# mLSTM scores in a hybrid decoder step: queries and their remainder side by side, one product of 256 columns a block

## The chip, the cores and the metric

The kernel runs on one core of a Trainium2 chip. A core has five engines that run on their own and meet through semaphores: TensorE (matmul; PE in the profile, its weight loads PEld), VectorE (DVE), ScalarE (ACT), GpSimd (POOL) and SyncE (SP, which here issues the DMAs). TensorE reads its operands from the on-chip memory SBUF and writes to the accumulator memory PSUM, which has eight banks of 512 fp32 columns; VectorE and ScalarE read PSUM and SBUF. The metric is the device time of one execution, in microseconds, as the median of several runs.

## The reference

One step of a 4-layer decoder trunk for a prompt of 512 tokens and 8 samples of 4 tokens each, all with width 1024. Layers 0 and 3 mix tokens with an mLSTM matrix memory, layer 1 with gated linear attention, layer 2 with sliding-window attention; each is followed by a convolutional feed-forward block. The part of the mLSTM mixer that the change touches, for the prompt, is the score product `qk` of a chunk (8 heads, 64 key channels a head):

```
logw = a[:, None, :, :] + (f_cum - m_t)[:, :, None, :]
w = jnp.where(causal, jnp.exp(jnp.minimum(logw, 0.0)), 0.0)
qk = jnp.einsum('bthd,bshd->btsh', q, k) * w
...
num = jnp.einsum('btsh,bshv->bthv', qk, v) + g[..., None] * jnp.einsum('bthd,bhdv->bthv', q, c)
den = jnp.sum(qk, axis=2) + g * jnp.einsum('bthd,bhd->bth', q, n)
h = num / jnp.maximum(jnp.abs(den), jnp.exp(-m_t))[..., None]
```

All arithmetic is fp32.

## The kernel before

**Number types.** TensorE takes a rounded fp32 type (fp32r). To keep fp32 accuracy, an operand is split into a rounded part and a remainder, and a product is made of several matmuls. All large matrices go this way: line 191 (ScalarE) makes the rounded weights `wh`, line 192 (VectorE) the remainder `wl`, and `gemm` (line 263) runs three products for each of two halves of 272 columns into the accumulator `acc`. Every matmul call stands at line 164, every transpose at line 167.

**Banks and scratch.** PSUM is divided into two double banks named `acc` (pool `psA`) for the large products, and four banks named `m` (pool `psM`) for everything else: scores, outputs of heads, carry, decode, transposes. SBUF has a pool of eight scratch tiles named `t`.

**Order of the work.** The program is written as one stream: `gemm` calls `tick` after each part, and `tick` advances generators (`attention`, line 902) that emit the token mixer's instructions in between. A planner then orders all instructions: it plays the program through with its own costs, takes of the instructions that can start the one that comes first in the program, and gives out tile buffers as they come free; weight conversions and evacuations (lines 190 and 243) get a raised priority. The order it finds is fixed for each engine; on the chip each engine works through its own list in order and waits on semaphores.

**mLSTM heads.** The prompt's 512 tokens are cut into four blocks of 128. For head `h`, with the heads of a pair in the two halves of 64 partitions:

- `decays(h)` (line 699) makes the weights `w` of the four blocks, 128x512, in the scratch tile `SW[h]`: four VectorE instructions (line 704) and an exponential on ScalarE (line 706).
- `prep(h)` (line 754) splits queries and keys. The 128 partitions hold 64 channels twice: `ks` has the rounded keys in one half and their remainder in the other, `qs` the rounded queries in both halves, `ql` the queries' remainder in both. So one matmul of `ks` against `qs` gives rounded and remainder keys times rounded queries, and one against `ql` the same for the remainder of the queries. There is one buffer of each (`bufs=1`), 128x512.
- `scores(h)` (line 767) takes one bank `m`; for each block two matmuls of 128 columns go to the same quarter of it, and the second accumulates on the first. VectorE multiplies the bank with `SW[h]` in place (line 774).
- `av(h)` (line 789) multiplies `SW[h]` with the values and the carried state into two banks, and works out norms and denominators: line 801 reads the denominators, line 783 squares (ScalarE, four a head), line 806 writes the scaled outputs and is the last to read the two banks.
- For each pair of heads, `carry_in` (line 716) transposes keys into a bank and weighs them, and `carry` (line 734) makes the state of the four blocks in two banks (sixteen narrow matmuls, read by lines 745 and 748). `dec_scores` and `dec_av` (lines 819 and 837) do the samples' tokens, `dec_av` with one bank.

Within the loop of `attention`, for each head: decode queries and scores (even heads), `decays` and `prep` of the next head, `carry_in` (odd heads), `av(h)`, then `scores(h + 1)`, behind it `carry` (odd heads) or, a tick later, `dec_av` (even heads), and at last `finish(h)`, which transposes the outputs. For each layer the first scores and the first carry come ahead of the loop.

Of the kernel before, what the change touches and what calls it, by code (L numbers as in the profile page):

```python
# [11 lines left out]
F32R = mybir.dt.float32r  # L12
I32 = mybir.dt.int32
AF = mybir.ActivationFunctionType
ALU = mybir.AluOpType
# [5 lines left out]
NP = 512  # L21
# [91 lines left out]
class Step:  # L113
# [433 lines left out]
    def mlstm(self, L, j):  # L547
        nc, a, tc = self.nc, self.a, self.tc
        ctx = ExitStack()
        mp = self.mp = ctx.enter_context(tc.tile_pool(name=f"mx{L}", bufs=1))  # L550
# [28 lines left out]
        Q, K = {}, {}  # L579
# [116 lines left out]
        SW = {}  # L696
# [55 lines left out]
        KQ = {}  # L752

        def prep(h):
            r = slice(64 * (h % 2), 64 * (h % 2) + 64)
            o = slice(64 - 64 * (h % 2), 128 - 64 * (h % 2))
            q, k = Q[h // 2][r, 0:NP], K[h // 2][r, 0:NP]
            ks, qs, ql = [mp.tile([128, NP], F32R, tag=x, name=x) for x in ("ks", "qs", "ql")]
            nc.scalar.activation(ks[r], k, AF.Copy)
            nc.scalar.activation(qs[r], q, AF.Copy)  # L760
            nc.scalar.activation(qs[o], q, AF.Copy)
            nc.vector.tensor_tensor(out=ks[o], in0=k, in1=ks[r].bitcast(F32), op=ALU.subtract)
            nc.vector.tensor_tensor(out=ql[r], in0=q, in1=qs[r].bitcast(F32), op=ALU.subtract)
            nc.scalar.activation(ql[o], ql[r].bitcast(F32), AF.Copy)
            KQ[h] = (ks, qs, ql)

        def scores(h):
            ks, qs, ql = KQ.pop(h)
            s = self.m()
            for i in range(4):  # L770
                c = slice(128 * i, 128 * i + 128)
                self.mm(s[:, c], ks[:, c], qs[:, c], True, False)
                self.mm(s[:, c], ks[:, c], ql[:, c], False, True)
            nc.vector.tensor_tensor(out=SW[h], in0=s, in1=SW[h], op=ALU.mult)

        def hnorm(num, den, ss, em, sc, cols, p, tag):

# [124 lines left out]
        def attention():  # L902
# [5 lines left out]
            yield 2  # L908
            decays(0)
            prep(0)  # L910
            carry_in(0)
            load_na(1)
            yield 2
            scores(0)
            yield 2
            carry(0)
            yield 2
            for h in range(8):
# [6 lines left out]
                if h + 1 < 8:  # L925
                    while ("qk", (h + 1) // 2) not in done:
                        yield 1
                    decays(h + 1)
                    prep(h + 1)
                    if h % 2:  # L930
                        carry_in(p + 1)
# [4 lines left out]
                if h + 1 < 8:  # L936
                    yield 1
                    scores(h + 1)
                    if h % 2:
                        carry(p + 1)  # L940
# [895 lines left out]
```

## Time and profile before

| | us |
|---|---|
| median of 3 runs | 2587.24 (2584.53 to 2589.8) |
| profiled execution | 2587.89 |
| its span, first to last instruction | 2586.1 |
| TensorE busy | 2554.6 (99%) |
| VectorE busy | 1594.1 (62%) |
| ScalarE busy | 1103.4 (43%) |
| GpSimd busy | 218.5 (8%) |

The busy time of an engine is the time in which at least one of its instructions runs; matmuls overlap, so that a matmul's own duration (some 0.28 us) is longer than the distance between the starts of two. In a row of a group, the figures behind the bar are busy time in us, mean duration of one in ns, and the idle time of the engine just before them with what ended it. In a row of a timeline, the first figure is the start in us from the span's start, the second the time from the start of the first to the end of the last of the merged instructions, and brackets at the end hold the idle time before it and what ended it. A row of waits names the waiting engine, its tile and line, behind the arrow the one that it waited for, then the total in us, how often, and the longest.

### The profile page before, as it was taken

The page shows a single profiled execution, that of the slowest core. Times are in us where ns is not written, and L with a number is a line of the kernel's source. Part 1 is how long each engine was busy: PE and PEld are TensorE (multiplying, and loading weights), DVE is VectorE, ACT ScalarE, POOL GpSimd, SP SyncE. Part 2 cuts the span into 40 slices and gives each one's busy share as a digit, 9 for nine tenths or more (in the row PEclk, how much of TensorE's full clock was granted, in tenths as well). Part 3 has the DMA queues.
Part 4 walks back from the last instruction along what each step waited for, and adds up shares of the span by engine and source line. Part 5 has one row for each costly group of instructions (what it writes and reads, how often), then busy time and mean ns, then how long its engine had stood idle before and what let it go on. Part 6 is the DMA issues. An engine that isn't in the chain of part 4 may idle for free.

```text
span 2586.1 us, 52775 instructions
## 1 busy us (share of the span) xinstructions
PE 2554.6 (99%) x21207; PEld 2499.3 (97%) x21207; DVE 1594.1 (62%) x3401; ACT 1103.4 (43%) x2092; POOL 218.5 (8%) x571
## 2 busy tenths in 40 slices
PE   8999999999999999999999999999999999999998
PEld 7999999999998899999999999999999999999998
DVE  5677775545457666564557865464555777756464
ACT  5544433334455543232347743232345544423232
POOL 2110000001002200000010000000010110000000
PEclk9999999999999999999999999999999999999999
DMA  5333333233222224433332223323333332333332
GB/s 178 105 106 81 91 111 103 84 93 99 74 79 88 91 84 143 139 92 88 88 115 67 69 71 89 87 87 90 86 101 101 100 93 82 111 111 85 91 85 81
DMA packets 137573, 247.24 MB, mean 96 GB/s; under 512 B 16528, under 2 KB 32400, under 8 KB 137296
## 3 DMA queue, kind: packets, MB, share of 16 engines
q1 hardware_dynamic: 135888, 242.26, 32.3%
q8 instruction: 167, 2.74, 0.4%
q10 hardware_dynamic: 1440, 1.60, 0.2%
q14 instruction: 78, 0.64, 0.1%
HBM read 230.89 MB, written 14.94 MB: 95 GB/s over the span
## 4 chain that ended last, share of the span: by engine, by line
PE 93%; DVE 4%; ACT 1%; issue 1%; DMA 1%; POOL 1%; DVEq 0%; SPq 0%; POOLq 0%; ACTq 0%
PE acc L164 81%; PE m L164 11%; PE m L167 1%; POOL s L544 0%; DVE wl L192 0%; DVE t L704 0%; ACT junk L783 0%; DMA out_a_cso<-st 0%; DVE t L513 0%; DMA XT<-in_x 0%; DVE sg L987 0%; DVE st L869 0%; ACT wh L191 0%; DVE t L1096 0%; DMA sd<-in_b_s 0%
## 5 line engine op out<-in xcount | busy, mean ns | idle before, releaser
L191 ACT ACTIVATE wh<-wr 128x512 fp32r<-128x512 f32 (+2 forms) x776 | 482.4, 623 | 1080.2 <-PE acc L164 986.3
L164 PE MATMUL acc<-XH,wh 128*128 128x272 f32 x3744 | 786.8, 291 | 0.0
L164 PE MATMUL acc<-XH,wl 128*128 128x272 f32 x3744 | 776.2, 288 | 0.0
L164 PE MATMUL acc<-XL,wh 128*128 128x272 f32 x3744 | 775.1, 288 | 0.0
L192 DVE TENSOR_TENSOR wl<-wr,wh 128x512 fp32r<-128x512 f32 (+2 forms) x776 | 523.4, 675 | 314.1 <-ACT wh L191 310.1
L164 PEld LDWEIGHTS acc<-XH,wh 128*128 128x128 f32 x3744 | 587.2, 188 | 8.3 <-issue 6.0
L164 PEld LDWEIGHTS acc<-XL,wh 128*128 128x128 f32 x3744 | 588.3, 188 | 1.0 <-issue 0.8
L164 PEld LDWEIGHTS acc<-XH,wl 128*128 128x128 f32 x3744 | 586.2, 189 | 1.1 <-issue 0.8
L164 PE MATMUL acc<-HH,wh 128*128 128x272 f32 x1920 | 404.5, 290 | 1.7 <-DVE sg L987 1.5
L164 PE MATMUL acc<-HL,wh 128*128 128x272 f32 x1920 | 399.1, 288 | 0.2 <-DVE HL L344 0.2
L164 PE MATMUL acc<-HH,wl 128*128 128x272 f32 x1920 | 398.7, 288 | 0.0
L164 PEld LDWEIGHTS acc<-HH,wh 128*128 128x128 f32 x1920 | 302.2, 188 | 4.8 <-DVE sg L987 2.0
L164 PEld LDWEIGHTS acc<-HL,wh 128*128 128x128 f32 x1920 | 302.4, 188 | 0.5 <-DVE HL L344 0.5
L164 PEld LDWEIGHTS acc<-HH,wl 128*128 128x128 f32 x1920 | 301.4, 189 | 0.0
L530 DVE TENSOR_TENSOR XT<-acc,XT 128x544 f32<-128x544 f32 x158 | 114.2, 723 | 137.9 <-PE acc L164 136.5
L443 POOL COPY cc<-t 128x2 f32<-128x2 f32 x88 | 54.6, 620 | 1283.9 <-DVE t L441 1278.7
L440 DVE TENSOR_TENSOR t<-acc,rb 128x272 f32<-128x272 f32 x88 | 38.9, 442 | 143.4 <-PE acc L164 140.7
L164 PE MATMUL m<-wh,XH 128*128 128x256 f32 (+1 forms) x400 | 115.5, 290 | 7.1 <-ACT XH L346 6.6
L164 PE MATMUL m<-wl,XH 128*128 128x256 f32 (+1 forms) x400 | 114.6, 287 | 1.0 <-DVE wl L192 1.0
L164 PE MATMUL m<-wh,XL 128*128 128x256 f32 (+1 forms) x400 | 114.6, 287 | 0.0
L455 DVE TENSOR_TENSOR t<-acc,t 128x544 f32<-128x544 f32 x88 | 63.7, 723 | 70.5 <-PE acc L164 69.9
L446 ACT ACTIVATE t<-t,par 128x560 f32<-128x560 f32 x88 | 75.4, 857 | 51.2 <-DVE t L442 51.2
(359 smaller groups left out, 2616.7 us busy)
## 6 DMA issues: line engine op xcount, KB each, us to landing
wr<-in_w SPq DMA_DIRECT2D x700, 256.0 KB
wr<-in_w SPq DMA_DIRECT2D x64, 192.0 KB
st<-in_a_cs SPq DMA_DIRECT2D x16, 520.0 KB
sd<-in_b_s SPq DMA_DIRECT2D x32, 256.0 KB
out_a_cso<-st SPq DMA_DIRECT2D x8, 520.0 KB
na<-scr SPq DMA_DIRECT2D x16, 256.0 KB
out_b_so<-sd SPq DMA_DIRECT2D x16, 256.0 KB
wr<-in_w SPq DMA_DIRECT2D x12, 272.0 KB
```

Of the source, the lines that this page charges most:

```text
L164: self.nc.tensor.matmul(out, lhsT=lhsT, rhs=rhs, start=start, stop=stop, skip_group_check=True, **kw)
L167: self.nc.tensor.transpose(out, in_, self.ident[0:k, 0:k])
L191: self.nc.scalar.activation(hi[:, 0:n], raw[:, 0:n], AF.Copy)
L192: self.nc.vector.tensor_tensor(out=lo[:, 0:n], in0=raw[:, 0:n], in1=hi[:, 0:n].bitcast(F32), op=ALU.subtract)
L440: nc.vector.tensor_tensor(out=g[:, 2:274], in0=acc[:, 0, 0:HT], in1=rb[:, 0:HT], op=ALU.mult)
L443: nc.gpsimd.tensor_copy(cout[:, f, 0:2], g[:, 512:514])
L446: nc.scalar.activation(c, g[:, 2:562], AF.Identity, scale=self.par[:, pw + 2:pw + 3], bias=self.par[:, pb:pb + 1])
L455: nc.vector.tensor_tensor(out=self.h2(h), in0=acc[:, :, 0:HT], in1=self.h2(s2), op=ALU.mult)
L530: self.nc.vector.tensor_tensor(out=self.h2(x), in0=acc[:, :, 0:HT], in1=self.h2(x), op=ALU.add)
```

## The change

`qs` and `ql` become the two halves of one tile `qq`, 128 x 4 blocks x 2 x 128: for each block the rounded queries and their remainder stand side by side. `ks` gets the shape 128 x 4 x 128. The six preparing instructions stay, with the new views as outputs. `scores` takes two banks, one for two blocks each: a block is one matmul of 256 columns, whose first 128 results come from the rounded queries and the second 128 from the remainder. The sum of the two, made by the second matmul's accumulation before, is made outside: ScalarE copies the remainder's half out of the bank into a new scratch tile `w`, VectorE adds the other half of the bank to it, each once a bank; then VectorE multiplies `w` with `SW[h]`.

```diff
         def prep(h):
             r = slice(64 * (h % 2), 64 * (h % 2) + 64)
             o = slice(64 - 64 * (h % 2), 128 - 64 * (h % 2))
-            q, k = Q[h // 2][r, 0:NP], K[h // 2][r, 0:NP]
-            ks, qs, ql = [mp.tile([128, NP], F32R, tag=x, name=x) for x in ("ks", "qs", "ql")]
+            q, k = [x[h // 2][r, 0:NP].rearrange("p (c x) -> p c x", c=4) for x in (Q, K)]
+            ks = mp.tile([128, 4, 128], F32R, tag="ks", name="ks")
+            qq = mp.tile([128, 4, 2, 128], F32R, tag="qq", name="qq")
+            qs, ql = qq[:, :, 0], qq[:, :, 1]
             nc.scalar.activation(ks[r], k, AF.Copy)
             nc.scalar.activation(qs[r], q, AF.Copy)
             nc.scalar.activation(qs[o], q, AF.Copy)
             nc.vector.tensor_tensor(out=ks[o], in0=k, in1=ks[r].bitcast(F32), op=ALU.subtract)
             nc.vector.tensor_tensor(out=ql[r], in0=q, in1=qs[r].bitcast(F32), op=ALU.subtract)
             nc.scalar.activation(ql[o], ql[r].bitcast(F32), AF.Copy)
-            KQ[h] = (ks, qs, ql)
+            KQ[h] = (ks, qq)
 
         def scores(h):
-            ks, qs, ql = KQ.pop(h)
-            s = self.m()
-            for i in range(4):
-                c = slice(128 * i, 128 * i + 128)
-                self.mm(s[:, c], ks[:, c], qs[:, c], True, False)
-                self.mm(s[:, c], ks[:, c], ql[:, c], False, True)
-            nc.vector.tensor_tensor(out=SW[h], in0=s, in1=SW[h], op=ALU.mult)
+            ks, qq = KQ.pop(h)
+            w = self.t(512).rearrange("p (a x) -> p a x", a=4)
+            for half in range(2):
+                s = self.m().rearrange("p (a b x) -> p a b x", a=2, b=2)
+                for i in range(2):
+                    c = 2 * half + i
+                    self.mm(s[:, i].rearrange("p b x -> p (b x)"), ks[:, c], qq[:, c].rearrange("p b x -> p (b x)"), True, True)
+                w2 = w[:, 2 * half:2 * half + 2]
+                nc.scalar.copy(w2, s[:, :, 1])
+                nc.vector.tensor_tensor(out=w2, in0=s[:, :, 0], in1=w2, op=ALU.add)
+            nc.vector.tensor_tensor(out=SW[h], in0=w.rearrange("p a x -> p (a x)"), in1=SW[h], op=ALU.mult)
```

## The prediction

> **What bounds the kernel now.** I read the page's busy rows and its chain first, then a table by stage for the two stretches in which the mLSTM heads are worked on, and then the waits of TensorE.
>
> ```profile
> span 2586.1 us, 52775 instructions
> PE 2554.6 (99%) x21207; PEld 2499.3 (97%) x21207; DVE 1594.1 (62%) x3401; ACT 1103.4 (43%) x2092; POOL 218.5 (8%) x571
> PE 93%; DVE 4%; ACT 1%; issue 1%; DMA 1%; POOL 1%; DVEq 0%; SPq 0%; POOLq 0%; ACTq 0%
> ```
> ```profile
> core 0: us, PE busy (x) PEld busy (x) DVE busy (x) ACT busy (x) POOL busy (x), PEclk, DMA share, GB/s
> 75.00:225.00 150.00, 146.95 (x1231) 140.02 (x1230) 108.23 (x313) 72.40 (x174) 18.25 (x23) 1.00 0.35 100
> 1990.00:2130.00 140.00, 136.94 (x1151) 130.01 (x1150) 101.82 (x299) 65.84 (x162) 16.87 (x21) 1.00 0.35 95
> ```
> ```profile
> PE m L164 <- DVE t L774: 2.5, 4, 1.1
> ```
>
> The reader sees a kernel that is TensorE's own stream of matmuls: 99% busy, 93% of the chain, and 147 of 150 us in the mLSTM stretch of layer 0. So whatever shortens that stream shortens the kernel one for one, and whatever makes TensorE wait lengthens it one for one. The clock is full in these stretches, so it is no variable. VectorE (108 of 150 us) and ScalarE (72 of 150) have room. The last row is where the changed code already touches TensorE: four times it stands still, 2.5 us in all, until the multiplication at line 774 has read the score bank. Each layer's stretch repeats the same order of instructions, so what happens once per layer counts twice.
>
> **The change, part by part.**
>
> *Matmuls.* Before, one head's scores are eight matmuls of 128 columns; the start times tell what one costs, since a matmul's own duration overlaps the next one's.
>
> ```profile
> 89.65 0.22 PE L164 MATMUL m<-qs,ks 128*128 128x128 f32 x1
> 89.71 0.27 PE L164 MATMUL m<-ql,ks 128*128 128x128 f32 x1
> ...
> 90.37 0.28 PE L164 MATMUL m<-ql,ks 128*128 128x128 f32 x1
> 90.49 0.46 PE L164 MATMUL acc<-XH,wh 128*128 128x272 f32 x2
> ```
> ```profile
> L164 PE MATMUL m<-qs,ks x64: 220/273/277, 89.6 to 2114.1; 128*128 128x128 f32 x64
> L164 PE MATMUL m<-ql,ks x64: 272/275/280, 89.7 to 2114.2; 128*128 128x128 f32 x64
> ```
>
> From 89.65 to 90.49 is 0.84 us for eight, some 0.11 us a step, and there are (64 + 64) / 8 = 16 such sets, eight in each mLSTM layer. What a 256-column step of the same number type costs stands in the attention layer, where the stationary side changes each time, as it will here:
>
> ```profile
> 1379.62 0.28 PE L164 MATMUL m<-KEL,qs 128*128 128x256 f32 x1
> ...
> 1381.26 0.27 PE L164 MATMUL m<-KOL,qs 128*128 128x256 f32 x1
> 1381.37 0.29 PE L164 MATMUL acc<-XH,wh 128*128 128x272 f32 x1
> ```
>
> From 1379.62 to 1381.37 these are 15 steps (the thirteen rows left out are of the same kind) in 1.75 us, 0.117 us each. A step of 256 columns thus costs hardly more than one of 128, and four of them cost 0.47 us. The saving is 0.84 - 0.47 = 0.37 us a set, 16 x 0.37 = **5.9 us**. Six sets are followed by the carry's narrow products and take 0.93 us (193.62 to 194.55 below); if the extra 0.09 us belongs to the scores, the saving is 6 x 0.09 = 0.5 us more. I take **6.2**, between 5.9 and 6.5. The number of weight loads falls with the matmuls; they lie beside them and are in the step already.
>
> One rule of the Trainium skill speaks against this term. "TensorE: Matmul & The Clock Gate", section "Back-to-back issue gap", gives the spacing of isolated matmuls as columns over 2.4 GHz plus 2.5 ns, an estimate of 56 ns for 128 columns and 109 ns for 256; by it eight narrow ones cost 0.45 us, four wide ones 0.44 us, and the change saves nothing. The trace disagrees: 0.84 us for the eight. The same page's section "LDWEIGHTS (loading the stationary operand)" charges a load of 128 columns with columns over 1.2 GHz, 107 ns, which as a floor under both kinds would give an estimate of 16 x (8 x 107 - 4 x 109) ns = 6.7 us; that is near the rows.
>
> *New work on ScalarE and VectorE.* For each set two copies (128x256, out of a bank) on ScalarE and two additions (128x256, one operand in a bank) on VectorE; the multiplication stays, and now reads no bank.
>
> ```profile
> L411 ACT COPY rb<-m 128x512 f32<-128x512 f32 x8 | 4.7, 586 | 4.0 <-PE m L164 3.9
> L745 ACT COPY cs<-m 128x129 f32<-128x129 f32 x8 | 2.1, 264 | 0.2
> L806 DVE TENSOR_TENSOR t<-m,s 128x256 f32<-128x256 f32 x32 | 12.2, 416 | 0.3
> L728 DVE TENSOR_TENSOR t<-m,Wc 128x256 f32<-128x256 f32 x16 | 6.0, 413 | 0.1
> L774 DVE TENSOR_TENSOR t<-m,t 128x512 f32<-128x512 f32 x16 | 11.0, 686 | 0.7 <-PE m L164 0.6
> L450 DVE TENSOR_TENSOR t<-t,rb 128x512 f32<-128x512 f32 x88 | 60.9, 692 | 8.2 <-ACT t L449 3.0
> ```
>
> A copy of 256 lies between 264 and 586 ns; on the straight line between them, 264 + 127/383 x 322 = 0.37 us. An addition is 0.416. So ScalarE gets 32 x 0.37 = 12 us more and VectorE 32 x 0.416 = 13 us more, half in each layer: VectorE's 108 becomes about 115 of 150, ScalarE's 72 about 78. TensorE's other products hide it; with that cover gone it would be up to 25 us. The multiplication is the same with a bank (686) or without (692). The six preparing instructions keep their number and size; only their output is now strided, and line 728, whose output is strided too, costs what line 806 with its contiguous one costs. Cost nothing, all of it. The queries' two tiles become one of the same total size. One scratch tile of the pool of eight is taken more per set: if none is free, ScalarE's copy waits, not TensorE, so between 0 and a share of the next term.
>
> *The banks, and who waits for them.* This is the uncertain term. There are four banks under the name m. When scores run, the head before still holds two (its outputs, until line 806). Scores took one and now take two, so **none is left**. Behind them in TensorE's queue come, by turns, the carry's products (eight times, two banks) and the decode products (eight times, one bank). A score bank is now free after copy and addition (0.37 + 0.42 us, on two queues), before it was after the multiplication (0.69, on one). How it goes today, at the seventh and the eighth set:
>
> ```profile
> 193.62 0.22 PE L164 MATMUL m<-qs,ks 128*128 128x128 f32 x1
> ...
> 194.55 0.88 PE L164 MATMUL m<-V,t 128*64 128x129 f32 x12
> ...
> 195.36 0.39 PE L164 MATMUL acc<-HH,wh 128*128 128x272 f32 x1
> ...
> 195.78 0.20 ACT L783 ACTIVATION_READ_ACCUMULATOR junk<-m 128x1 f32 x1
> ...
> 196.09 0.69 DVE L774 TENSOR_TENSOR t<-m,t 128x512 f32<-128x512 f32 x1
> ...
> 196.83 0.44 PE L164 MATMUL m<-V,t 128*64 128x129 f32 x4 [1.08 <-DVE t L774]
> ```
> ```profile
> 209.22 1.10 PE L164 MATMUL m<-st,qz 128*64 128x129 f32 x16
> ...
> 210.42 0.20 ACT L783 ACTIVATION_READ_ACCUMULATOR junk<-m 128x1 f32 x1
> ```
>
> Twelve of the carry's products go at once into the free bank; the last four need the score bank and come 1.08 us late. The decode products at 209.22 find a bank free. The planner puts big products ahead of whatever it expects to be blocked, so TensorE only loses what a bank is later than planned. Today that is 2.5 us over the six carries that come with two banks held (each layer's first has none held), 0.42 each. Afterwards 14 followers (6 carries, 8 decodes) hang on a score bank. Lower bound: lateness vanishes in the new order, 0 and the old 2.5 regained. Upper bound: two queues in place of one double it, 14 x 0.84 = 11.8, 9.3 more than now. I take the lateness as it is now, since planner and queues are the same: 14 x 0.42 = 5.9, less the 2.5 paid already, **+3.4 us**.
>
> Sum: -6.2 + 3.4 = **-2.8 us**. The profiled execution took 2587.89 (span 2586.1 and 1.8 around it), 0.65 above the runs' median of 2587.24; the difference carries over: 2587.24 - 2.8 = **2584.4 us**.
>
> **The rivals.** About 0.2% (5.2 us) is what a measurement of this kernel can tell from no change.
>
> *The whole saving stays.* The planner knows the banks' state, and may move all carries and decodes far enough back. For it: TensorE always has other products here, and only four of the present followers wait visibly. Against it: today's lateness of up to 1.08 us at a place planned in the same way. Time: between -6.2 and -8.7 with the old 2.5 gone, about -7.0, 2580.2.
>
> *The copies queue behind the squares.* ScalarE works in order, and the four squares of the head before (line 783) stand around this place:
>
> ```profile
> L783 ACT ACTIVATE junk<-m 128x128 bf16<-128x128 f32 x64 | 17.5, 274 | 9.5 <-DVE s L801 8.2
> L783 ACT ACTIVATION_READ_ACCUMULATOR junk<-m 128x1 f32 x64 | 12.5, 195 | 0.1
> ```
>
> They take 4 x (274 + 195) ns = 1.9 us. At the seventh set they end at 195.98; copy and addition behind them free the first bank at 196.8, no sooner than today's multiplication did (196.78). But the twelve carry products (0.75 us) that lie in this time today would have to wait too, so a carry loses 0.42 + 0.75 = 1.17. At the eighth set squares end at 210.62 and the bank is free at 211.4, 2.2 us after today's decode products; half of it covered by planned products leaves 1.1. Together 6 x 1.17 + 8 x 1.1 = 15.8, less 2.5, less 6.2: +7.1, 2594.3. It decides from an average of (5.2 + 6.2 + 2.5) / 14 = 0.99 us a follower. Against it: squares are not always ahead; often other work stands between them, and the planner sees them.
>
> *The wide matmul costs twice the narrow one*, so nothing is saved: 2587.24 + 3.4 = 2590.6, no change by the bound. The spacing of 0.117 us at 256 columns speaks against it; only a property of this product's layout could bring it. The Trainium skill's isolated spacing ("TensorE: Matmul & The Clock Gate", "Back-to-back issue gap": 56 and 109 ns) would be this case.
>
> **How the numbers follow.** Forecast 0.52 (own range 2582 to 2589, all within 0.2%), whole saving 0.28, squares 0.15, wide matmuls dear 0.05. So faster 0.28, same 0.52 + 0.05 = 0.57, slower 0.15. The range leaves out about a tenth on either side: 2579.5 cuts the lower part of the whole saving, 2592.5 keeps what lies below the squares' full price.
>
> **What would show it.** The score rows: 64 matmuls of 128x256 where 128 stood, four starts some 0.117 us apart; 0.22 there means the wide ones are dear. TensorE's waits: a row for the addition's bank in place of line 774, under 6 us in all for the forecast, near 0 for the whole saving, over 14 for the squares, and then with a copy that stands behind line 783 in time. ScalarE's copies at 0.37 and the additions at 0.42. The forecast is wrong if the end moves by more than 5.2 us either way, or if the time goes to stages without mLSTM heads.

## The result, and the profile after

The changed kernel takes 2606.78 us (median of 4 runs, 2598.87 to 2608.1), the kernel before in the same series 2585.89 (2583.96 to 2589.8). The ratio is 1.007 with a 95% interval from 1.0057 to 1.0082: slower by about 20 us, where 2584.4 and no change was forecast, and beyond the range's 2592.5.

The page of the changed kernel, its rows of busy time and of the chain:

```profile
span 2605.8 us, 52720 instructions
PE 2554.3 (98%) x21143; PEld 2498.7 (96%) x21143; DVE 1609.1 (62%) x3433; ACT 1113.1 (43%) x2124; POOL 216.3 (8%) x571
PE 91%; DVE 4%; ACT 2%; issue 1%; DMA 1%; POOL 1%; DVEq 0%; SPq 0%; POOLq 0%; ACTq 0%
```

TensorE runs 64 matmuls fewer and is as long busy as before; its idle time has grown, and a share of its matmuls ran slower. Where, the table by stage says for the two stretches with mLSTM heads (columns: busy time of each engine, granted TensorE clock, DMA share, rate), and the waits of TensorE:

```profile
core 0: us, PE busy (x) PEld busy (x) DVE busy (x) ACT busy (x) POOL busy (x), PEclk, DMA share, GB/s
75.00:240.00 165.00, 152.53 (x1256) 145.40 (x1255) 117.92 (x337) 79.93 (x198) 17.43 (x24) 0.99 0.34 95
1990.00:2150.00 160.00, 147.46 (x1192) 140.13 (x1191) 111.81 (x317) 74.40 (x183) 15.89 (x22) 0.97 0.32 93
```
```profile
PE m L164 <- DVE t L812: 22.2, 12, 2.1
```

Line 812 is line 806 of the kernel before: VectorE's scaling of a head's outputs, the last to read that head's two banks (the lines behind the change have moved by six). TensorE stands before it twelve times, 1.85 us each. The 2.5 us of waits for the scores' multiplication are gone. So the followers do not wait for the score banks, as the prediction had it, but for the two banks of the **head before**. The timeline of the second set of scores shows why:

```profile
97.86 0.64 PE L164 MATMUL m<-qq,ks 128*128 128x256 f32 x4
98.33 0.41 PE L164 MATMUL acc<-XH,wh 128*128 128x272 f32 x2
...
99.40 0.62 ACT L762 ACTIVATE qq<-q 64x512 fp32r<-64x512 f32 x1
...
102.12 0.63 ACT L766 ACTIVATE qq<-qq 64x512 fp32r<-64x512 f32 x1
...
102.76 0.65 ACT L778 COPY t<-m 128x256 f32<-128x256 f32 x2
...
104.08 0.75 DVE L812 TENSOR_TENSOR t<-m,s 128x256 f32<-128x256 f32 x2
...
104.76 1.10 PE L164 MATMUL m<-st,qz 128*64 128x129 f32 x16 [1.75 <-DVE t L812]
...
105.38 0.74 DVE L779 TENSOR_TENSOR t<-m,t 128x256 f32<-128x256 f32 x2
...
106.64 0.68 DVE L780 TENSOR_TENSOR t<-t 128x512 f32<-128x512 f32 x1
```

The four wide matmuls start at 97.86 and cost 0.47 us, as forecast. Their copies start at 102.76, 4.4 us after the next product's start, although ScalarE has meanwhile prepared queries of the following head (99.40, 102.12), which stand later in the program. The copies do not wait on the chip: they follow line 766 without a gap, and line 812 writes only after them. What is late is their place in ScalarE's list, which the planner fixed. Until the additions at 105.38 both score banks are held. The decode products at 104.76 therefore had to take a bank of the head before, free after the first half of the scaling at 104.08, and TensorE stood for 1.75 us. The first set of a layer, with no head before it, has its copies 0.53 us behind the first matmul; in the fourteen others they come 4.1 to 7.3 us behind:

```profile
89.71 0.64 PE L164 MATMUL m<-qq,ks 128*128 128x256 f32 x4
...
90.24 0.63 ACT L778 COPY t<-m 128x256 f32<-128x256 f32 x2
```

The second loss is the clock. Behind the wait that ends at 129.76:

```profile
129.76 1.12 PE L164 MATMUL m<-V,t 128*64 128x129 f32 x16 [2.12 <-DVE t L812]
...
131.21 1.06 PE L167 MATMUL m<-cst,t 128*128 128x128 f32 x4
```
```profile
130.00:130.60 0.60, 0.60 (x16) 0.60 (x12) 0.60 (x2) 0.00 (x0) 0.00 (x0) 1.00 0.00 0
130.80:134.00 3.20, 3.20 (x14) 2.74 (x13) 3.06 (x7) 0.15 (x1) 0.00 (x0) 0.50 0.01 3
134.30:136.00 1.70, 1.70 (x15) 1.51 (x13) 0.38 (x3) 0.00 (x0) 0.00 (x0) 1.00 0.65 161
```

From about 130.7 to 134.1 the granted clock is 0.50, and then full again. Three more such pieces stand in the second stretch; the kernel before has none in either. Each piece lasts 3.41 us, so the four cost 4 x 3.41 x 0.5 = 6.8 us (by the table, whose clock is rounded, (1 - 0.99) x 165 + (1 - 0.97) x 160 = 6.5).

The sum, with the forecast's figure for the wide matmuls: -6.2, waits 22.2 - 2.5 = +19.7, clock +6.8, together +20.3; the spans differ by 2605.8 - 2586.1 = 19.7.

### The profile page after: what moved, and what is told of

It is laid out like the page before. It is cut to its first block, busy times and chain, and to the rows that moved or that the text cites. A ratio compares the mean times of both kernels' runs of the same rounds, so it can differ in the third digit from the quotient of the medians.

```text
span 2605.8 us, 52720 instructions
## 1 busy us (share of the span) xinstructions
PE 2554.3 (98%) x21143; PEld 2498.7 (96%) x21143; DVE 1609.1 (62%) x3433; ACT 1113.1 (43%) x2124; POOL 216.3 (8%) x571
## 4 chain that ended last, share of the span: by engine, by line
PE 91%; DVE 4%; ACT 2%; issue 1%; DMA 1%; POOL 1%; DVEq 0%; SPq 0%; POOLq 0%; ACTq 0%
PE acc L164 78%; PE m L164 11%; PE m L167 1%; POOL s L544 1%; ACT junk L789 0%; DVE wl L192 0%; DMA st<-in_a_cs 0%; ACT wh L191 0%; DVE t L704 0%; DVE t L812 0%; DMA wr<-in_w 0%; DVE st L875 0%; DMA XT<-in_x 0%; DVE t L513 0%; ACT qq L762 0%
```

## The experiments

Theory S: in the pool of scratch tiles, `w` gets its place only behind the scaled outputs of the head before (line 812 is their first write, and it stands ahead of the copies in the program). So the copies come late, the score banks stay held, and the followers hang on the head before. Rivals: B, two banks for the scores are too many by themselves; F, the pool of eight is full; P, the new layout costs; C, the late copies cost by way of ScalarE and VectorE. Ratios are to the kernel before in the same series, with 95% intervals.

**1. A buffer of its own for `w`.**

```diff
-            w = self.t(512).rearrange("p (a x) -> p a x", a=4)
+            w = mp.tile([128, XW], F32, tag="x1", name="sw")[:, 0:512].rearrange("p (a x) -> p a x", a=4)
```

(The tag `x1` is otherwise used by the feed-forward block alone, behind the mixer.)

> The changed kernel, with the scratch tile w of the scores taken from a buffer of its own instead of the pool of eight scratch tiles. Theory S (scratch order: w gets its place in the pool only behind the scaled outputs of the head before, so the copies come some 4 us late, the score banks stay held, and TensorE has to wait for the banks of the head before): the copies follow the scores within 2 us, TensorE's waits for the scaling at line 812 fall from 22 us to under 4, the time is 2578 to 2588. Theory B (two banks for the scores are by themselves too many): the waits stay near 22 us and the time near 2606.

Measured: 2585.93 us, ratio 0.9996 (0.9987 to 1.0006): the 20 us are gone, and no gain over the kernel before is left. Timeline of the second set, then the waits:

```profile
96.80 0.64 PE L164 MATMUL m<-qq,ks 128*128 128x256 f32 x4
97.23 0.37 ACT L778 COPY sw<-m 128x256 f32<-128x256 f32 x1 [1.95 <-PE m L164]
...
97.64 0.42 DVE L779 TENSOR_TENSOR sw<-m,sw 128x256 f32<-128x256 f32 x1
...
98.12 1.10 PE L164 MATMUL m<-st,qz 128*64 128x129 f32 x16
```
```profile
PE m L167 <- DVE t L812: 6.4, 4, 1.7
...
PE m L167 <- DVE hnd L859: 3.4, 3, 1.6
```

ScalarE now waits for the score product, makes the first copy at once, and the decode products start 1.3 us after the scores without a wait. Line 812 still appears, but in another place: the waiting line is 167, the transposes at a head's end, which read the scaled outputs. 6.4 us is more than the expected 4. No row of TensorE's waits names a score bank. B falls, S holds for the 20 us; what took the gain of the wide matmuls is asked in 6 and 7.

**2. The pool of eight, touched early.**

```diff
         def prep(h):
...
-            KQ[h] = (ks, qq)
+            w = self.t(512).rearrange("p (a x) -> p a x", a=4)
+            nc.gpsimd.memset(w[:, 0, 0:1], 0.0)
+            KQ[h] = (ks, qq, w)
```

> The changed kernel, with w still from the pool of eight, but touched once (one column set to zero by GpSimd) in prep, which stands ahead of the head before's scaled outputs in the program. Theory S: the order in the pool decides, so this is as good as a buffer of its own, waits under 4 us, 2578 to 2588. Theory F (the pool of eight is simply full, so that w has to wait for a tile to come free): w is held even longer, nothing is gained, 2600 to 2615. Theory B: 2606.

Measured: 2586.15 us, 1.0 (0.999 to 1.0009). `w` comes from the same pool of eight and is held longer, and still the loss is gone. F falls: one tile more held for longer costs nothing, and the place in the order in which the tiles are given out decides. How the planner came to the late place is read from the program's order and these two runs; a larger pool was not run. The waits are those of the buffer of its own, again above the expected 4:

```profile
PE m L167 <- DVE t L813: 6.4, 4, 1.7
```

**3. Two banks, nothing else.**

```diff
-            s = self.m()
-            for i in range(4):
...
-            nc.vector.tensor_tensor(out=SW[h], in0=s, in1=SW[h], op=ALU.mult)
+            for half in range(2):
+                s = self.m()
+                for i in range(2):
+                    c = slice(256 * half + 128 * i, 256 * half + 128 * i + 128)
+                    d = slice(128 * i, 128 * i + 128)
+                    self.mm(s[:, d], ks[:, c], qs[:, c], True, False)
+                    self.mm(s[:, d], ks[:, c], ql[:, c], False, True)
+                w2 = SW[h][:, 256 * half:256 * half + 256]
+                nc.vector.tensor_tensor(out=w2, in0=s[:, 0:256], in1=w2, op=ALU.mult)
```

> The kernel before, with its eight narrow matmuls spread over two banks, and the multiplication done once a bank (two of 128x256); no copy, no addition, no scratch tile. It is the bank shortage alone. Theory S: banks come free after one short VectorE instruction, the waits of TensorE stay under 6 us, the time is 2585 to 2592. Theory B: the followers wait for the banks of the head before as in the changed kernel, 2598 to 2608.

Measured: 2585.72 us, 0.9998 (0.9989 to 1.0008). TensorE's waits for the multiplication (line 777 here) are 3.5 us, against 2.5 with one bank. Holding the second bank for the length of one short instruction costs a microsecond of waits, which the time does not show. With the first kernel, which holds both banks through copy and addition as well, B is out.

```profile
PE m L164 <- DVE t L777: 3.5, 6, 0.8
```

**4. The layout alone.** `prep` as changed; `scores` with eight matmuls of 128 columns, `ks[:, i]` against `qq[:, i, 0]` and `qq[:, i, 1]`, into one bank.

> The kernel before with the new tile for queries and remainder side by side, but scores as before: eight narrow matmuls into one bank, accumulated there. Theories S and B: the layout costs nothing, 2584 to 2589. Theory P (strided outputs of the preparing instructions, or the joint tile's later release, cost time): 2592 or more.

Measured: 2587.03 us, 1.0001 (0.9991 to 1.001), with the same 2.5 us of waits as before. P falls.

**5. The followers later, the scratch tile as the change has it.**

```diff
                     scores(h + 1)
+                    yield 8
                     if h % 2:
                         carry(p + 1)
...
-                yield FY
+                yield 4
```

> The changed kernel with its scratch tile where the change put it, but the carry and the decode products are issued eight ticks (some 6 us) later behind the scores, and the head's end four ticks later in place of six. Theory S with lateness (the loss is TensorE standing at followers whose bank comes later than the order of work assumed): with the followers behind the time at which the bank really is free, their waits fall from 22 us to under 5 and the time returns to 2582 to 2592, though the copies stay late. Theory C (the late copies cost by themselves, by way of ScalarE and VectorE): the time stays above 2598.

Measured: 2587.82 us, 1.0004 (0.9994 to 1.0013). The copies are as late as in the changed kernel; the second set's scores start at 97.44, its multiplication at 106.23:

```profile
97.44 0.64 PE L164 MATMUL m<-qq,ks 128*128 128x256 f32 x4
...
104.78 1.10 PE L164 MATMUL m<-st,qz 128*64 128x129 f32 x16
...
106.23 0.68 DVE L780 TENSOR_TENSOR t<-t 128x512 f32<-128x512 f32 x1
```
```profile
PE m L164 <- DVE t L812: 8.5, 8, 2.0
```

The decode products start 7.3 us behind the scores, when the bank is free, and nothing stands. The waits fall to 8.5 us, more than the expected 5 (1.9 us more stand at line 167), and the time is back. So C falls: 12 us of work on ScalarE and an 8 us detour of the scores cost nothing by themselves that can be told. The loss was TensorE at the head of its own queue, standing for a bank that came later than the order of work had placed it.

**6 to 10. Where the gain of the wide matmuls went.** All but the control have `w` in a buffer of its own, save 10, which has it touched early. `FY` is the number of ticks between a head's outputs and its end, 6 in the kernel before and in the changed one.

```diff
-LY, FY = 2, 6
+LY, FY = 2, 8
```

> The changed kernel with w in a buffer of its own, and eight ticks in place of six between a head's outputs and its end (the transposes of the scaled outputs). The waits that took the place of the banks' in the first of the kernels with its own buffer are four of 1.6 us at these transposes. Theory S: they vanish, 2577 to 2584, faster than before by some 0.2%. Rival (the wait moves on to another place, the order is late there too): 2584 to 2589.

Measured: 2577.91 us, 0.9966 (0.9955 to 0.9978).

```profile
PE m L167 <- DVE hnd L859: 4.9, 4, 1.5
...
PE m L167 <- DVE t L812: 1.4, 2, 0.7
```

The transposes' waits for line 812 fall from 6.4 to 1.4 us, those for line 859 rise from 3.4 to 4.9: together from 9.8 to 6.3, 3.5 us less, so each expectation holds in part. The rest is clock. The first kernel's profile has two pieces at 0.50 in the mLSTM stretches, at 128.7 and 2108.4 us, this one has none: 2 x 3.41 x 0.5 = 3.4 us. Together that is 6.9; the medians of the spans differ by 2582.95 - 2576.1 = 6.9. The kernel is faster than before.

Priority instead of ticks: `hnorm` and the scaling behind it under `with tc.high_priority(offset=100)`, `FY` at 6.

> The changed kernel with w in a buffer of its own, and the chain from a head's outputs to their scaling (denominators, squares, norms, line 812) at raised priority in the order of work. Theory S: the scaling is no longer late, the transposes wait less (under 3 us), 2577 to 2584. Rival (the lateness is in the durations, not in the order): waits stay near 6 us, 2584 to 2589.

Measured: 2592.03 us, 1.0024 (1.0015 to 1.0033): slower, which neither expectation held.

```profile
PE m L167 <- DVE t L813: 6.7, 4, 1.8
...
PE m L167 <- DVE hnd L860: 4.5, 4, 1.4
```

The waits stay: 11.2 us in these two rows, against 9.8 with the buffer of its own alone. The rest is clock, 0.994 granted over the span against 0.996, which is 2589.5 x 0.006 - 2582.3 x 0.004 = 5.2 us; with the 1.4 us of waits that makes 6.6 of the 6.1 between the two medians (the clock's rows are rounded). Moving the chain up in the order by this much does not help. Why the scaling comes when it does, and which of its instructions takes longer than the order of work assumes, isn't shown by a run here.

The control, the kernel before with `FY = 8`:

> The kernel before with eight ticks in place of six between a head's outputs and its end, as a control: all theories, 2583 to 2588, no change that can be told.

Measured: 2586.32 us, 0.9997 (0.9987 to 1.0006): eight ticks alone gain nothing.

`FY = 10` with `w` in a buffer of its own:

> The changed kernel with w in a buffer of its own and ten ticks between a head's outputs and its end. If the gain of the version with eight ticks is the saving of the wide matmuls (6 us) with the waits out of the way, ten ticks do as well, 2576 to 2583. If it is one lucky order of instructions, this one falls back to 2584 to 2589.

Measured: 2572.86 us, 0.9946 (0.9931 to 0.9961), the fastest kernel of the study, 14 us below the kernel before, and below the expected range.

`FY = 8` with `w` from the pool, touched early:

> The changed kernel with w from the pool of eight but touched early, and eight ticks between a head's outputs and its end. Same question: 2576 to 2583 if the gain is the wide matmuls', 2584 to 2589 if it is one lucky order.

Measured: 2579.64 us, 0.997 (0.9958 to 0.9981). Three orders with the waits out of the way (8 and 10 ticks, and the other place for `w`) gain, so it isn't one lucky order.

**11 and 12. How much of it is the ticks' own.** The kernel before with `FY = 10`:

> The kernel before with ten ticks between a head's outputs and its end: how much of the gain of the version with ten ticks is the ticks' own. Theory W (the wide matmuls' 6 us are the larger part): 2578 to 2587. Rival (the ticks are all of it): 2570 to 2576.

Measured: 2581.45 us, 0.9985 (0.9975 to 0.9994): ten ticks alone are worth some 5 us. That is why `FY = 10` with its own buffer fell below its range. It is 2581.45 - 2572.86 = 8.6 us below this one. (The spans of the profiled executions differ by only 2579.3 - 2573.1 = 6.2, but the profiled one of the faster kernel was the slowest of its four, 2574.95.) At eight ticks the like difference is 2586.32 - 2577.91 = 8.4 us.

`FY = 12` with `w` in a buffer of its own:

> The changed kernel with w in a buffer of its own and twelve ticks. All theories: the waits at the end of a head are gone with ten, so nothing more is won, 2571 to 2577; if the heads now end too late for the products behind them, 2577 to 2590.

Measured: 2574.9 us, 0.9958 (0.9942 to 0.9975): nothing more to win.

## Why the prediction was wrong, point by point

**The bound, and TensorE one for one: right.** The kernels whose times moved show it in TensorE's waits, its granted clock or its matmuls.

**The matmuls, -6.2 us: right, and rather too small.** In the timeline above four wide matmuls cost 98.33 - 97.86 = 0.47 us, where 0.47 was worked out. With the same ticks the kernels differ by 8.4 us at eight and 8.6 at ten; TensorE's busy time at eight, both at a clock of 0.997, falls from 2553.8 to 2546.7, by 7.1. What makes the one to two us beyond 6.2 isn't shown. The rival of the dear wide matmuls falls. The Trainium skill's isolated spacing ("TensorE: Matmul & The Clock Gate", "Back-to-back issue gap") would have made this term nothing, and these rows are against it too.

**The copies and additions: right.** Foreseen 0.37 and 0.416 us:

```profile
L778 ACT COPY t<-m 128x256 f32<-128x256 f32 x32 | 10.1, 366 | 0.0
L779 DVE TENSOR_TENSOR t<-m,t 128x256 f32<-128x256 f32 x32 | 11.9, 414 | 0.0
```

They are hidden, as was said; the fifth kernel hides them in spite of the detour. The layout costs nothing (fourth kernel).

**The scratch tile: this step failed.** The prediction put it as "if none is free, ScalarE's copy waits, not TensorE, so between 0 and a share of the next term". It asked whether one of eight was free, not in which order they are given out; and it stopped at ScalarE, without asking what the waiting copy holds. The late copy holds two banks, and TensorE waits for banks. In the first and second kernel the price of this one line is 2606.78 - 2586 = some 20 us.

**The banks: the bound rested on the wrong bank.** +3.4 us, at most 9.3, came from scaling the lateness of the score bank (0.42 us). With the score banks held, the followers got the banks of the head before, whose chain of ten steps over three engines ends 1.85 us late on average, four times as much. With score banks given back promptly the term is smaller than +3.4: the third kernel pays 1 us more, and the first one, which has the whole change without the scratch order, has no wait for a score bank at all. That the first one ends near the forecast, 0.7 us under the kernel before where 2.8 under was forecast, is luck: the gain of its matmuls goes to places that the sum did not have, 9.8 us of waits at the transposes (2.0 before) and two pieces at half clock.

**The clock "is no variable": wrong.** It was full before in these stretches, where TensorE's longest wait was 1.1 us. Behind waits of 1.9 to 2.1 us came 6.8 us on top.

**The slower rival** had the right place (copies behind other work on ScalarE, held banks, followers standing) and the wrong cause and size: not only the squares but the next head's preparation runs ahead of the copies, and its price of +7.1 counted neither the other bank nor the clock.

## What to carry to other kernels

A tile from a shared pool has a place in an order as well as a size: before taking one more, ask what stands ahead of it in the pool, and what its first writer holds while it waits. When an accumulator bank stays held for longer, look up which bank the next user gets instead and what ends that one's chain. A gain on the bounding engine shows only when the waits that the new order brings are moved out of its way: here 0 with six ticks, 9 us with eight, 14 with ten, of which 5 are the ticks' own.

## What was not expected of the hardware

Waits of 2 us and less were followed by half the clock. The trace's record of the granted clock has the four pieces at 0.50 in the changed kernel's mLSTM stretches begin at 130.71, 2045.59, 2062.66 and 2086.55 us, each 3.413 us long. The distances between them are 561, 5 and 7 times that length, so they stand on one fixed grid. The four fields of the grid just ahead of them hold 2.12, 2.13, 1.89 and 2.05 us of waiting. The wait of 2.04 us that ends at 169.34 is cut by the grid into 0.95 and 1.08, and no piece follows; no other field in these stretches holds more than 1.83. So in this kernel a wait's place on the grid counts beside its length.

Length and place are not all. In the kernel with a buffer of its own (first experiment) a wait of 1.53 us is followed by a piece:

```profile
127.63 0.68 PE L167 MATMUL m<-cst,t 128*128 128x128 f32 x4 [1.53 <-DVE t L812]
```
```profile
128.80:132.00 3.20, 3.20 (x18) 2.89 (x17) 3.11 (x11) 0.89 (x2) 0.00 (x0) 0.50 0.24 44
```

The like wait of the other layer, 1.53 us that ends at 2032.52 and also lies in one field, is followed by none. And a piece at 1448.26 in the changed kernel, in the attention layer, follows no wait; the kernel before has one at 1489.36. What decides there stays open.

The Trainium skill, "TensorE: Matmul & The Clock Gate", section "Why this matters for your kernels", advises to have no idle gaps above about 3 us. The trace differs: 1.5 to 2.1 us sufficed here, at some places. The same page's section "What's actually happening" tells of a window of 3.4 us that runs freely; the grid of 3.413 us agrees with it.

The spread of the changed kernel fits it: three runs of 2606 to 2608 us had 0.994 to 0.995 of the clock, the one of 2598.87 had 0.998, and 0.003 of 2600 us is 8 us.
